# A hybrid decoder layer: where the first FFN weights and the last norms stand among the out-projection's products, and which engine takes the samples' small FFN steps

## The chip, the cores and the metric

The kernel runs on one core of one Trainium2 chip. The metric is device time in microseconds (us) of one execution. A core has five engines that each work through their own queue in order: TensorE (PE, matrix products, with PEld for its weight loads), VectorE (DVE), ScalarE (ACT), GpSimd (POOL) and SyncE (SP, which here issues nearly all DMAs).

## What is computed

One layer of a decoder for 2048 prompt tokens and for 32 sample tokens (8 sequences of 4), model width 1024. Four mixers share one input projection; their normed outputs are concatenated, and the rest of the layer is what this change touches:

```python
x = x + jnp.concatenate([ya, yb, yc, yd], axis=-1) @ P['w_out'][l]
hn = rmsnorm(x, P['norm_ffn_g'][l])
x = x + jnp.square(jax.nn.relu(hn @ P['w_up'][l])) @ P['w_down'][l]
...
y_prompt = rmsnorm(h, norm_final_g)
```

All is float32 in and out. The kernel makes each fp32 operand into a high and a low fp16 part and does three fp16 products for one fp32 product.

## The kernel before

**Planner.** The program is written against a framework that plans the order of the instructions on each engine when the kernel is built: an instruction written earlier has priority over one written later, and the planner, with its own estimates of durations, lets each engine take the ready instruction of the highest priority. On the chip that order is fixed, so an engine stands still when the instruction at its head isn't ready. Tiles of one tag share a number of buffers (`bufs`); a tile's first writer waits until the last user of the buffer's previous tile is done.

**Out-projection** (`outproj`, from L1864). Prompt tokens are worked on in units of 256 (a pair of 128-token tiles), two units to a block; blocks 0 and 1 go first and are put aside in DRAM, then blocks 2 and 3 (`BLOCKS[0]`) follow. `load` (L1883) fetches a unit's `cat` (tag `cat`, 2 buffers) and its residual `x2`. `product(cat, x2, t, m)` (L1892) makes 512 of the 1024 output columns of one token tile: 48 products of 256 columns into one PSUM tile `px` (2 buffers), then two adds on DVE (L1898). `m = 0` uses the weight tiles `W[0]`, `W[1]`, `m = 2` uses `W[2]`, `W[3]`; these four tiles fill the four buffers of tag `w`, in which the FFN's `wd` and `wdT` tiles must later find a place. For block 3 all four `m = 0` products stand ahead of all four `m = 2` products, and after them both units' `norm_pair`.

**Norm** (`norm_pair`, L1939). For each token tile: sum of squares on ACT (L1950), reciprocal root on POOL (L150, L151), scaling on DVE (L1953, `xn`), eight transposes on PE (L144), copies from PSUM on ACT (L1958) into `xt`. `combine` (L1960) makes the operand forms of a Strassen-like product of 2x2 blocks: four subtractions into `tt` (L1964 to L1967; for block 3 L1965 is on POOL), then high parts on ACT (L1971) and low parts on DVE (L1972) into `hn`. For block 3 `xt` and `tt` are tiles of tag `cat`, so they take the two buffers that the units' `cat` leave; the FFN's `fr` (L2076) has the same tag and comes after them.

**FFN weights.** `ffn_wu(s, c)` (L2008) loads 256 columns of `w_up` into a staging tile `ws` (2 buffers, shared with the norms of block 2), and for `s = 0` finds a power-of-two scale: squares on ACT (L183), a product with ones on PE (`pd<-w_ss,ones`), one POOL step (L188) and small DVE steps (L187, L155, L191, L192). Then it makes high parts on ACT (L176) and low parts on DVE (L177), with four POOL steps on `ws` between (L2027 to L2030). `ffn_wd(s, c)` (L2036) does the same for 256 rows of `w_down` (POOL steps L2053 to L2056, tiles `wd` and `wdT`).

**FFN** (`ffn`, L2061). Pass `s = 0` works on blocks 2 and 3 and the samples, pass `s = 1` on blocks 0 and 1. In a pass, 16 chunks `c` of 256 hidden columns, each for both blocks: 64 steps in all. `up` makes seven products of 12 matrix instructions each, evacuated by ACT (L2089, L2107) and DVE (L2092) into `fr`, then relu and square on ACT (L2111, L2112), and the forms `ht` of the second Strassen-like product (POOL L2129 to L2131, L2137, L2139, L2140; ACT and DVE). `down` makes 14 groups of three 512-column products and adds them into the residual on DVE (L2182), scaled by `f`. A step's `up` is written ahead of the previous step's `down`. The samples ride along with block 2 (272 instead of 256 columns); for them `hs` holds high and low parts of the squared values: four ACT steps (L2119) and four DVE steps (L2120) per chunk, read by 32 small products (`pd<-hs,wd`) that DVE adds to `accs` (L2157). `f` is made once per chunk and pass from the scales by three DVE steps on one column (L2220 to L2222).

**Order around the change.** `ffn_wu(0, 0)` is written ahead of block 2's norms. `ffn_wd(0, 0)` is the first thing in `ffn`, after both norms of block 3. `ffn_wu(0, 1)` comes in the main loop at `n = 0`, after `up` of the first two steps.

Of the kernel before, what the change touches and what calls it, by code (L numbers as in the profile page):

```python
# [10 lines left out]
F16 = mybir.dt.float16  # L11
BF = mybir.dt.bfloat16
I32 = mybir.dt.int32
AF = mybir.ActivationFunctionType
OP = mybir.AluOpType
# [8 lines left out]
NS = 32  # L24
# [3 lines left out]
BLOCKS = [(2, 3), (0, 1)]  # L28
# [75 lines left out]
class K:  # L104
# [1763 lines left out]
    def outproj(self, ctx, mix):  # L1868

        nc, A = self.nc, self.A  # L1870
        W = self.Wo
        self.fp = ctx.enter_context(self.pool("ffn", 1))
        self.hnp = ctx.enter_context(self.pool("hn0", 1))
        gb, self.ish, g8 = self.gain_row(self.hnp, A["norm_ffn_g"], "ffn", True)

        self.xp = {BLOCKS[0][0]: ctx.enter_context(self.pool("x2a", 1))}
        rot = mix.enter_context(self.pool("rot", 2, "right"))

        self.xD = {b: [self.dr.tile([128, 2 * D], F32, name=f"x2D{b}{i}") for i in range(2)] for b in BLOCKS[1]}
        self.hD = {b: [self.dr.tile([128, 7 * 4 * 2 * 128], F16, name=f"hnD{b}{i}") for i in range(2)] for b in BLOCKS[1]}  # L1880

        def load(u, b, i):

            cat = self.hnp.tile([128, 8, 2, 256], F16, name="cat", tag="cat", bufs=2)
            for g in range(4):
                nc.sync.dma_start(cat[:, 2 * g:2 * g + 2], self.catD[g][u // 2][:, :, :, u % 2 * 256:u % 2 * 256 + 256])
            x2 = self.xp[b].tile([128, 2, D], F32, name="x2", tag=f"x2{b}{i}")
            nc.sync.dma_start(x2, A["x_prompt"][0, u * 256:(u + 1) * 256, :].rearrange("(i p) d -> p i d", p=128))
            return cat, x2

        def product(cat, x2, i, m):

            p = self.ps("mm", [128, 512])
            for mm in range(2):
                self.proj_tok(p[:, mm * 256:(mm + 1) * 256], cat[:, :, :, i * 128:i * 128 + 128], W[m + mm][0], 0, 256)
            for mm in range(2):
                o = x2[:, i, (m + mm) * 256:(m + mm + 1) * 256]
                nc.vector.scalar_tensor_tensor(o, p[:, mm * 256:(mm + 1) * 256], W[m + mm][1], o, op0=OP.mult, op1=OP.add)  # L1898

        for b in BLOCKS[1]:  # L1900
            for i in range(2):
                cat, x2 = load(2 * b + i, BLOCKS[0][0], i)
                for t in range(2):
                    for m in (0, 2):
                        product(cat, x2, t, m)
                hn = rot.tile([128, 7, 4, 2, 128], F16, name="hnr")
                self.norm_pair(x2, gb, hn)
                nc.sync.dma_start(self.xD[b][i], x2.rearrange("p t d -> p (t d)"))
                nc.sync.dma_start(self.hD[b][i], hn.rearrange("p o k a n -> p (o k a n)"))
        first = [load(2 * BLOCKS[0][0] + i, BLOCKS[0][0], i) for i in range(2)]  # L1910
        for i, t, m in ((i, t, m) for i in range(2) for t in range(2) for m in (0, 2)):
            product(*first[i], t, m)
        mix.close()
        self.xp[BLOCKS[0][1]] = ctx.enter_context(self.pool("x2b", 1, "right"))
        self.hp = ctx.enter_context(self.pool("hn", 1))
        self.bank["t"] = "b"
        self.wup = ctx.enter_context(self.pool("wu", 2, "right"))
        self.wts = {}
        self.accs = self.hp.tile([128, 8, NS], F32, name="accs")
        self.wsc = self.hp.tile([128, 2, 4096 // FC, 2], F32, name="wsc")  # L1920
        self.x2, self.hn = {}, {}
        for b in BLOCKS[0]:
            n = 128 + (NS // 4 if b == BLOCKS[0][0] else 0)
            hn = self.hp.tile([128, 2, 7, 4, 2, n], F16, name=f"hn{b}", tag=f"hn{b}")
            prs = first
            if b != BLOCKS[0][0]:
                prs = [load(2 * b + i, b, i) for i in range(2)]

                for i, t, m in ((i, t, m) for m in (0, 2) for i in range(2) for t in range(2)):
                    product(*prs[i], t, m)  # L1930
            if b == BLOCKS[0][0]:
                self.ffn_wu(0, 0)
            for i in range(2):
                self.norm_pair(prs[i][1], gb, hn[:, i, :, :, :, 0:128], b == BLOCKS[0][1])
            if b == BLOCKS[0][0]:
                self.out_sample(hn, g8)
            self.x2[b] = [x2 for _, x2 in prs]
            self.hn[b] = hn

# [121 lines left out]
    def ffn(self):  # L2061
        nc, A, O = self.nc, self.A, self.O
        RS = float(0.7 * 2.0 ** -20)
# [1 line left out]
        nc.sync.dma_start(gf, dram(A["norm_final_g"], 0, [[0, 128], [1, D]]))  # L2065
        accs = self.accs
        NC_ = 4096 // FC
        self.ffn_wd(0, 0)

        def up(s, c, b):  # L2070

# [2 lines left out]
            n = X.shape[5]  # L2074
            N = 2 * n
            r2 = self.hnp.tile([128, 7, N], F32, name="fr", tag="cat", bufs=2)  # L2076
            C, S = r2[:, 0:4], r2[:, 4:7]
            p, q, r = self.ps("s", [128, 512]), self.ps("mm", [128, 512]), self.ps("mm", [128, 512])
# [29 lines left out]
            for i in range(4):  # L2108
                x = C[:, i, :]
# [2 lines left out]
                nc.scalar.activation(x, x, AF.Square)  # L2112
            hs = None
            if n > 128:
                hs = self.hp.tile([128, 2, 2, 2, 2, 8], F16, name="hs", bufs=2)
                for m in range(2):
                    for t in range(2):
                        x = C[:, ((0, 2), (3, 1))[m][t], :].rearrange("p (i n) -> p i n", i=2)[:, :, 128:]
                        nc.scalar.activation(hs[:, m, 0, t], x, AF.Copy)  # L2119
                        nc.vector.tensor_sub(hs[:, m, 1, t], x, hs[:, m, 0, t])  # L2120


            ht = self.fp.tile([128, 7, 2, N], F16, name="ht", tag="xn", bufs=2)
# [20 lines left out]
        def down(s, c, b, ht, f):  # L2144
            ht, hs = ht
            n = ht.shape[3] // 2
            wd = self.wts[s, c][2]
            if hs is not None:
                p = self.ps("o", [128, 8, 2, NS])
                for m in range(8):  # L2150
                    for k in range(2):

                        x, o = hs[:, k].rearrange("p a t i n -> p (a t i n)"), p[:, m].rearrange("p a n -> p (a n)")
                        self.mm(o, wd[:, k, 0, m * 128:(m + 1) * 128], x, start=m + k == 0, stop=False)
                        self.mm(o[:, 0:NS], wd[:, k, 1, m * 128:(m + 1) * 128], x[:, 0:NS], start=False, stop=k == 1)
                for a in range(2):
                    nc.vector.scalar_tensor_tensor(accs, p[:, :, a, :], f, accs, op0=OP.mult, op1=OP.add)  # L2157
                if c == NC_ - 1:
                    self.ffn_sample_out(gf)
            for i in range(2):  # L2160
                if (s, c) in PLAIN:
                    down_plain(wd, self.x2[b][i], ht[:, :, :, i * n:i * n + 128], f)
                else:
                    down_pair(wd, self.wts[s, c][3], self.x2[b][i], ht[:, :, :, i * n:i * n + 128], f)
                if c == NC_ - 1:
                    for t in range(2):
                        tok = (4 * b + 2 * i + t) * 128
                        self.final(self.x2[b][i][:, t, :], 128, gf, O["y_prompt"][0, tok:tok + 128, :],
                                   (b, i) != (BLOCKS[1][1], 1))
# [42 lines left out]
        steps = [(s, c, b) for s in range(2) for c in range(NC_) for b in BLOCKS[s]]  # L2212
        first = BLOCKS[0][0]
        ht, f = up(*steps[0]), None
        for n, (s, c, b) in enumerate(steps):
            if b == BLOCKS[s][0]:

                _, iu, _, _, idn = self.wts[s, c]
                f = self.col("ff", bufs=4)
                nc.vector.tensor_scalar(f, iu, self.ish, 1.0 / RS, op0=OP.mult, op1=OP.mult)  # L2220
                nc.vector.tensor_mul(f, f, f)
                nc.vector.tensor_mul(f, f, idn)  # L2222
            nx = up(*steps[n + 1]) if n + 1 < len(steps) else None
            if (s, c) != (1, NC_ - 1):
                (self.ffn_wu if b == BLOCKS[s][0] else self.ffn_wd)(s + (c + 1) // NC_, (c + 1) % NC_)
            down(s, c, b, ht, f)
            if s == 0 and c == NC_ - 1:
                self.ffn_load(b, BLOCKS[1][BLOCKS[0].index(b)])
            ht = nx
# [66 lines left out]
```

## Time and profile before

| | |
|---|---|
| time, median of 3 runs | 2596.7 us (2593.09 to 2603.4) |
| the profiled execution | 2600.62 us |
| its span, first to last instruction | 2598.8 us |
| mean granted TensorE clock over the span | 0.974 of full speed |
| out-projection ends, FFN begins | about 1293 us |
| pass 0 of the FFN ends | about 1957 us |

A view by windows gives the busy time of each engine in a stretch, with its instruction count in brackets, then the granted TensorE clock (PEclk, 1.00 is full speed), the share of time that the DMA engines were busy and what they moved. Timeline rows give start, duration, engine, line, operation, output and inputs, count, and in square brackets how long the engine had been idle just before and what released it. Rows by line give busy time and mean nanoseconds, then the idle time of the engine just before such instructions and what ended it.

### The profile page before, as it was taken

To read this page: it belongs to the slowest core of one execution; us is meant where nothing else is said; L and a number is where in the kernel's file an instruction comes from. 1 tells how busy PE (TensorE), PEld (TensorE's weight loads), DVE (VectorE), ACT (ScalarE), POOL (GpSimd) and SP (SyncE) were. 2 spreads that over 40 slices of the span, in tenths; PEclk is the share of its full clock that TensorE was granted. 3 is DMA by queue.
4 is the path that set the end of the run, shared out by engine and by line. 5 is a ranking of instruction groups with operands and counts; after the bars stand their busy time and mean duration, and the time that the engine had idled before them with its cause. 6 is when DMAs were issued, how large, how long until landed. Compare 5 with 4: busy or idle time off the path is not lost.

```text
span 2598.8 us, 51309 instructions
## 1 busy us (share of the span) xinstructions
PE 2433.9 (94%) x20492; PEld 1660.2 (64%) x20492; DVE 2007.0 (77%) x3742; ACT 1312.5 (51%) x2449; POOL 1214.8 (47%) x1265
## 2 busy tenths in 40 slices
PE   6989999999999899999979999999998999999997
PEld 5875554454467677689856666666665666666664
DVE  5666667875566777654689998898997898999996
ACT  6544333033346677562455565556556554555554
POOL 3503122223214566540255555556556665666652
PEclk9989999999999998999989999999999999999999
DMA  6333416879722433355111111121136211121101
GB/s 190 96 73 94 89 40 199 301 256 336 254 87 75 132 104 97 99 175 212 52 41 50 60 55 50 49 66 33 55 126 216 77 59 50 56 66 49 66 33 65
DMA packets 209464, 278.31 MB, mean 107 GB/s; under 512 B 42852, under 2 KB 177121, under 8 KB 198952
## 3 DMA queue, kind: packets, MB, share of 16 engines
q1 hardware_dynamic: 199848, 207.40, 25.7%
q0 software_dynamic: 9376, 67.64, 7.2%
q8 instruction: 160, 2.62, 0.4%
q14 instruction: 80, 0.66, 0.1%
HBM read 217.85 MB, written 54.29 MB: 105 GB/s over the span
## 4 chain that ended last, share of the span: by engine, by line
PE 53%; DVE 17%; POOL 13%; ACT 6%; issue 5%; DMA 5%; SPq 1%; POOLq 0%; DVEq 0%; ACTq 0%
PE pb L140 26%; PE px L140 24%; DVE x L2182 4%; DVE wu L177 2%; PE pd L140 2%; DVE wd L177 1%; PE pb L144 1%; POOL ht L2137 1%; DMA ws<-in_w_up_dram 1%; POOL ws L2030 1%; POOL ws L2028 1%; POOL ht L2139 1%; POOL ws L2029 1%; DVE wdT L177 1%; ACT wdT L176 1%
## 5 line engine op out<-in xcount | busy, mean ns | idle before, releaser
L140 PEld LDWEIGHTS <-wu 128*128 128x128 f16 x5376 | 529.7, 99 | 225.9 <-issue 40.9
L2182 DVE SCALAR_TENSOR_TENSOR x<-pb,ff,x 128x512 f32<-128x512 f32 x840 | 591.3, 740 | 27.0 <-PE pb L140 23.0
L140 PE MATMUL px<-hn,wu 128*128 128x256 f16 (+1 forms) x3072 | 427.2, 276 | 16.6 <-DVE hn L1972 7.6
L140 PEld LDWEIGHTS <-ht 128*128 128x128 f16 x2712 | 264.1, 98 | 231.5 <-issue 25.0
L140 PE MATMUL pb<-wdT,ht 128*128 128x512 f16 x1440 | 379.6, 381 | 16.0 <-DVE x L2182 9.1
L140 PE MATMUL px<-xT,w 128*128 128x512 f16 (+1 forms) x1968 | 368.0, 338 | 1.5 <-ACT da L722 1.2
L140 PE MATMUL pb<-wd,ht 128*128 128x512 f16 x1272 | 336.0, 381 | 6.5 <-DVE x L2182 4.9
L140 PE MATMUL pb<-hn,wu 128*128 128x256 f16 (+1 forms) x2304 | 303.3, 277 | 16.7 <-DVE x L2182 8.4
L140 PEld LDWEIGHTS <-w 128*128 128x128 f16 x2160 | 167.4, 99 | 184.8 <-issue 25.1
L900 POOL TENSOR_TENSOR pl<-P,ph 128x512 f16<-128x512 f32 (+3 forms) x160 | 166.4, 1049 | 159.6 <-ACT ph L897 65.7
L176 ACT ACTIVATE wu<-ws,wsc 128x1024 f16<-128x1024 f32 (+1 forms) x128 | 129.4, 1036 | 128.7 <-POOL ws L2030 76.6
L177 DVE SCALAR_TENSOR_TENSOR wu<-ws,wsc,wu 128x1024 f16<-128x1024 f32 (+1 forms) x128 | 169.9, 1341 | 17.5 <-ACT wu L176 17.3
L140 PE MATMUL px<-w,cat 128*128 128x256 f16 x1536 | 180.2, 274 | 3.3 <-DMA cat<-cat 3.3
L140 PE MATMUL px<-w,xT 128*128 128x128 f16 (+1 forms) x2400 | 155.2, 223 | 15.5 <-DVE xT L402 8.0
L140 PEld LDWEIGHTS <-cat 128*128 128x128 f16 x1536 | 149.6, 98 | 25.7 <-DMA cat<-cat 3.4
L140 PEld LDWEIGHTS <-xT 128*128 128x128 f16 (+1 forms) x2672 | 151.3, 100 | 21.9 <-DVE xT L402 11.3
L893 ACT ACTIVATE P<-pb,nck,cc 128x512 f32<-128x512 f32 (+3 forms) x160 | 112.2, 710 | 76.0 <-PE pb L140 73.4
L2134 ACT ACTIVATE ht<-fr 128x1024 f16<-128x1024 f32 (+1 forms) x60 | 64.2, 1070 | 160.3 <-POOL fr L2140 160.2
L2137 POOL TENSOR_TENSOR ht<-fr,ht 128x512 f16<-128x512 f32 (+1 forms) x60 | 83.2, 1386 | 113.7 <-ACT ht L2136 112.4
L2053 POOL TENSOR_TENSOR ws<-ws 128x512 f32<-128x512 f32 x30 | 40.5, 1349 | 187.7 <-DVE wd L177 187.7
L862 DVE TENSOR_REDUCE mx<-pb 128x1 f32<-128x512 f32 (+3 forms) x160 | 94.9, 607 | 41.5 <-PE pb L140 40.2
L2111 ACT ACTIVATE fr<-fr 128x256 f32<-128x256 f32 (+1 forms) x192 | 77.0, 414 | 93.4 <-DVE fr L2092 92.5
(713 smaller groups left out, 4650.1 us busy)
## 6 DMA issues: line engine op xcount, KB each, us to landing
ws<-in_w_up_dram SPq DMA_DIRECT2D x32, 1024.0 KB
ws<-in_w_down_dram SPq DMA_DIRECT2D x32, 1024.0 KB
ws<-in_w_in_dram SPq DMA_DIRECT2D x22, 512.0 KB
x<-in_x_prompt_dram SPq DMA_DIRECT2D x16, 512.0 KB
cat<-cat SPq DMA_DIRECT2D x32, 256.0 KB
x<-in_x_prompt_dram SPq DMA_DIRECT2D x8, 1024.0 KB
out_y_prompt_dram<-x SPq DMA_DIRECT2D x32, 256.0 KB
hnD<-hnr SPq DMA_DIRECT2D x4, 1792.0 KB
```

The lines of the kernel that those rows point to most:

```text
L140: self.nc.tensor.matmul(out, lhsT, rhs, start=start, stop=stop, skip_group_check=True)
L144: self.nc.tensor.transpose(out, in_, self.ident[:n, :n])
L176: self.nc.scalar.activation(hi, x, AF.Copy, scale=sc)
L177: self.nc.vector.scalar_tensor_tensor(lo, x, sc, hi, op0=OP.mult, op1=OP.subtract)
L862: nc.vector.tensor_reduce(mx[:, ii, jb:jb + 1], s[:, :n], axis=AX.X, op=OP.max)
L893: nc.scalar.activation(P[:, :n], s[:, :n], AF.Exp, bias=nck[:, j, h, kt:kt + 1], scale=cc[:, h // 2:h // 2 + 1])
L900: (nc.gpsimd if 1 else nc.vector).tensor_sub(pl[:, :n], P[:, :n], ph[:, :n])
L2053: nc.gpsimd.tensor_sub(B11, B12, B11)
L2111: nc.scalar.activation(x, x, AF.Relu)
L2134: nc.scalar.activation(ht[:, o:o + m, 0, :], x, AF.Copy)
L2137: nc.gpsimd.tensor_sub(ht[:, 0:2, 1, :], C[:, 0:2, :], ht[:, 0:2, 0, :])
L2182: nc.vector.scalar_tensor_tensor(o, p, f, o, op0=OP.mult, op1=OP.add)
```

## The change

Four things. In `outproj`, block 3's steps are written in another order: four `m = 0` products, `ffn_wd(0, 0)`, the first unit's two `m = 2` products, its norm, `ffn_wu(0, 1)`, the second unit's two `m = 2` products, its norm. Accordingly `ffn_wd(0, 0)` leaves `ffn`, and the main loop no longer makes `ffn_wu(0, 1)` at `n = 0`. In `up`, the samples' high and low parts are made for two of the four blocks at a time, so two ACT steps and two low-part steps per chunk in place of four and four; the low-part steps go from DVE to POOL, and the order of the dimensions in `hs` is changed to suit, with `down`'s small products reading the same columns. The three steps for `f` go from DVE to POOL.

```diff
@@ outproj
             prs = first
-            if b != BLOCKS[0][0]:
-                prs = [load(2 * b + i, b, i) for i in range(2)]
-
-                for i, t, m in ((i, t, m) for m in (0, 2) for i in range(2) for t in range(2)):
-                    product(*prs[i], t, m)
             if b == BLOCKS[0][0]:
                 self.ffn_wu(0, 0)
-            for i in range(2):
-                self.norm_pair(prs[i][1], gb, hn[:, i, :, :, :, 0:128], b == BLOCKS[0][1])
-            if b == BLOCKS[0][0]:
+                for i in range(2):
+                    self.norm_pair(prs[i][1], gb, hn[:, i, :, :, :, 0:128])
                 self.out_sample(hn, g8)
+            else:
+                prs = [load(2 * b + i, b, i) for i in range(2)]
+                for i, t in ((i, t) for i in range(2) for t in range(2)):
+                    product(*prs[i], t, 0)
+                self.ffn_wd(0, 0)
+                for i in range(2):
+                    for t in range(2):
+                        product(*prs[i], t, 2)
+                    self.norm_pair(prs[i][1], gb, hn[:, i, :, :, :, 0:128], True)
+                    if i == 0:
+                        self.ffn_wu(0, 1)
@@ ffn
-        self.ffn_wd(0, 0)
@@ up
-                hs = self.hp.tile([128, 2, 2, 2, 2, 8], F16, name="hs", bufs=2)
-                for m in range(2):
-                    for t in range(2):
-                        x = C[:, ((0, 2), (3, 1))[m][t], :].rearrange("p (i n) -> p i n", i=2)[:, :, 128:]
-                        nc.scalar.activation(hs[:, m, 0, t], x, AF.Copy)
-                        nc.vector.tensor_sub(hs[:, m, 1, t], x, hs[:, m, 0, t])
+                hs = self.hp.tile([128, 2, 4, 2, 8], F16, name="hs", bufs=2)
+                for q in range(2):
+                    x = C[:, 2 * q:2 * q + 2, :].rearrange("p o (i n) -> p o i n", i=2)[:, :, :, 128:]
+                    d = [hs[:, a, q:4 - q:3 - 2 * q] for a in range(2)]
+                    nc.scalar.activation(d[0], x, AF.Copy)
+                    nc.gpsimd.tensor_sub(d[1], x, d[0])
@@ main loop
-                nc.vector.tensor_scalar(f, iu, self.ish, 1.0 / RS, op0=OP.mult, op1=OP.mult)
-                nc.vector.tensor_mul(f, f, f)
-                nc.vector.tensor_mul(f, f, idn)
+                nc.gpsimd.tensor_scalar(f, iu, self.ish, 1.0 / RS, op0=OP.mult, op1=OP.mult)
+                nc.gpsimd.tensor_mul(f, f, f)
+                nc.gpsimd.tensor_mul(f, f, idn)
             nx = up(*steps[n + 1]) if n + 1 < len(steps) else None
-            if (s, c) != (1, NC_ - 1):
+            if (s, c) != (1, NC_ - 1) and n > 0:
```

## Rows read from the trace of the kernel before

**Rows 1.** The page's part 1: busy time, share of the span and instructions by engine.

```profile
PE 2433.9 (94%) x20492; PEld 1660.2 (64%) x20492; DVE 2007.0 (77%) x3742; ACT 1312.5 (51%) x2449; POOL 1214.8 (47%) x1265
```

**Rows 2.** Windows: turn to the FFN, most of pass 0, most of pass 1.

```profile
1293.00:1375.00 82.00, 59.38 (x435) 43.21 (x434) 67.00 (x85) 50.09 (x85) 49.42 (x40) 0.88 0.12 39
1375.00:1957.00 582.00, 554.86 (x4125) 371.12 (x4125) 528.83 (x847) 337.88 (x598) 328.00 (x306) 0.99 0.19 61
2050.00:2560.00 510.00, 504.45 (x3451) 338.32 (x3450) 466.54 (x617) 253.77 (x469) 304.87 (x261) 0.99 0.16 52
```

**Rows 3.** Windows: last out-projection products, and the two stretches after them.

```profile
1278.00:1293.00 15.00, 15.00 (x140) 13.47 (x138) 4.91 (x8) 6.08 (x8) 1.46 (x4) 1.00 0.24 71
1293.00:1300.00 7.00, 4.48 (x40) 3.96 (x38) 4.79 (x11) 6.53 (x10) 3.69 (x5) 1.00 0.02 4
1300.00:1328.40 28.40, 12.10 (x61) 8.70 (x62) 27.93 (x22) 14.59 (x17) 19.72 (x12) 0.64 0.06 25
```

**Rows 4.** Timeline, 1278 to 1295 us: `wd`'s squares, a scaled token tile, then PE.

```profile
1278.35 1.91 ACT L183 ACTIVATE wd<-ws 128x2048 f16<-128x2048 f32 x1 [2.71 <-DMA ws<-in_w_down_dram]
...
1287.01 1.28 DVE L1953 SCALAR_TENSOR_TENSOR xn<-x,n_rstd,gb 128x1024 f32<-128x1024 f32 x1 [2.61 <-POOL n_rstd L151]
...
1292.83 1.91 PE L144 MATMUL pb<-cst,xn 128*128 128x128 f32 x16
...
1294.58 0.28 PE L140 MATMUL pd<-w_ss,ones 128*128 128x1 f32 x2
```

**Rows 5.** Timeline, 1317 to 1329 us: PE's longest waits and the first evacuations into `fr`.

```profile
1317.85 2.29 PE L140 MATMUL px<-hn,wu 128*128 128x256 f16 x10 [7.55 <-DVE hn L1972]
...
1324.73 0.38 ACT L2089 ACTIVATE fr<-px 128x272 f32<-128x272 f32 x1
...
1324.87 3.14 PE L140 MATMUL pb<-hn,wu 128*128 128x256 f16 x14 [4.74 <-ACT hn L1971]
```

**Rows 6.** By line, 1375 to 1957 us, PE: what it waited for before products.

```profile
L140 PE MATMUL pb<-wdT,ht 128*128 128x512 f16 x684 | 180.1, 380 | 8.6 <-DVE x L2182 8.4
L140 PE MATMUL pb<-hn,wu 128*128 128x256 f16 (+1 forms) x1044 | 140.4, 279 | 10.4 <-DVE x L2182 7.4 <-ACT fr L2089 2.9
L140 PE MATMUL pb<-wd,ht 128*128 128x512 f16 x519 | 138.0, 379 | 5.2 <-DVE x L2182 4.9
```

**Rows 7.** By line, whole span: low parts of weights on DVE.

```profile
L177 DVE SCALAR_TENSOR_TENSOR wu<-ws,wsc,wu 128x1024 f16<-128x1024 f32 (+1 forms) x128 | 169.9, 1341 | 17.5 <-ACT wu L176 17.3
...
L177 DVE SCALAR_TENSOR_TENSOR wdT<-ws,wsc,wdT 128x2048 f16<-128x2048 f32 x30 | 74.1, 2471 | 10.5 <-ACT wdT L176 10.5
```

**Rows 8.** By line, whole span: DVE steps that the change moves.

```profile
L2120 DVE TENSOR_TENSOR hs<-fr,hs 128x16 f16<-128x16 f32 x64 | 33.6, 531 | 11.8 <-ACT hs L2119 11.8
...
L2221 DVE TENSOR_TENSOR ff<-ff 128x1 f32<-128x1 f32 x32 | 15.6, 490 | 0.2
...
L2222 DVE TENSOR_TENSOR ff<-ff,wsc 128x1 f32<-128x1 f32 x32 | 13.2, 412 | 0.3
```

**Rows 9.** By line, whole span: one of the POOL steps on staged weights.

```profile
L2030 POOL TENSOR_TENSOR ws<-ws 128x512 f32<-128x512 f32 x32 | 58.1, 1816 | 1.7
```

**Rows 10.** Timeline of PE in an earlier block: a norm's transposes among products.

```profile
1202.63 0.60 PE L144 MATMUL pd<-cst,xn 128*128 128x128 f32 x4
```

**Rows 11.** By tile (`ff`, `hs`): nanoseconds min/median/max, first and last start.

```profile
L2220 DVE TENSOR_SCALAR ff<-wsc,inv_ffn x32: 195/202/215, 1242.1 to 2456.7; 128x1 f32<-128x1 f32 x32
...
L2120 DVE TENSOR_TENSOR hs<-fr,hs x64: 157/513/1267, 1331.3 to 1946.6; 128x16 f16<-128x16 f32 x64
```

**Rows 12.** Small two-input POOL steps: by tile (min/median/max), and by line and shape.

```profile
L2261 POOL TENSOR_TENSOR fi_rs<-fi_ssq x17: 183/193/2241, 1977.0 to 2591.5; 128x1 f32<-128x1 f32 x16, 32x1 f32<-32x1 f32 x1
...
L1231 POOL TENSOR_TENSOR qCe<-qeA,xbcS 128x64 f32<-128x64 f32 x2 | 0.6, 320 | 0.0
```

**Rows 13.** Timeline, 1377 us: last low part of a chunk's `hs`, then its product.

```profile
1377.20 0.16 DVE L2120 TENSOR_TENSOR hs<-fr,hs 128x16 f16<-128x16 f32 x1
...
1377.97 0.75 PE L140 MATMUL pd<-hs,wd 128*128 128x64 f16 x22
```

More of the change, by code (lines that the diff above doesn't have):

```diff
@@ L2151, in down @@
                     for k in range(2):
-                        x, o = hs[:, k].rearrange("p a t i n -> p (a t i n)"), p[:, m].rearrange("p a n -> p (a n)")
+                        x, o = hs[:, :, 2 * k:2 * k + 2].rearrange("p a t i n -> p a (t i n)"), p[:, m]
                         self.mm(o, wd[:, k, 0, m * 128:(m + 1) * 128], x, start=m + k == 0, stop=False)
-                        self.mm(o[:, 0:NS], wd[:, k, 1, m * 128:(m + 1) * 128], x[:, 0:NS], start=False, stop=k == 1)
+                        self.mm(o[:, 0], wd[:, k, 1, m * 128:(m + 1) * 128], x[:, 0], start=False, stop=k == 1)
                 for a in range(2):
```

## The prediction

> **What bounds the kernel now.** First, part 1 of the page: TensorE is busy for 94% of the span and no other compute engine for more than 77% [rows 1], so time is to be gained only where PE stands still or runs at the low clock. The windows say where that is [rows 2]. In the turn from out-projection to FFN, 1293 to 1375 us, PE is busy for 59.4 of 82 us: 22.6 us idle, at a mean granted clock of 0.88. In pass 0 of the FFN it is idle for 582 - 554.9 = 27.1 us, in pass 1 for 510 - 504.5 = 5.5 us. The change touches just these three stretches.
>
> The turn, read closer: while the last products run, 1278 to 1293, PE is full, but DVE works for 4.9 us of 15, ACT for 6.1 and POOL for 1.5 [rows 3]. Right after it is the other way round: from 1300 to 1328.4 DVE is busy for 27.9 of 28.4 us and PE for 12.1, at a mean granted clock of 0.64, a mixture of its two levels (1.2 and 2.4 GHz) after PE had begun to wait. The timeline shows why so little was done ahead. The squares of `wd` were finished at 1280.3 and the second scaled token tile of the first unit at 1288.3, but the transposes and the product with ones that go on from them stand on PE at 1292.8 and 1294.6, behind all products [rows 4]. After that PE waits 7.55 us for low parts of `hn` and 4.74 us for high parts, and the first evacuation into `fr` is at 1324.73 [rows 5], since `fr` takes a buffer that `xt` has to leave.
>
> In pass 0 three rows hold 24.2 us of PE's idle time, and 8.4 + 7.4 + 4.9 = 20.7 us of it ended with the residual adds of L2182 on DVE, which free PSUM [rows 6].
>
> **The change part by part.**
>
> *Order of block 3.* No instruction is removed; some 20 us of DVE, ACT and POOL work gets a higher priority than the last products, or than half of them. Of DVE's work after 1293 four things can be done before: the split of `wd` (2.5 us by the 2471 ns of a step of that size), the low parts of the first unit from `xt` and the first splits of `wu` (0, 1) (two steps each of 1.34 us or less), and the split of `wdT` when its POOL steps are through [rows 7]. That is 6 to 9 us, and DVE has 15 - 4.9 = 10 us free there [rows 3]. `tt` can't come forward: its buffer is the second unit's `cat`, in use until the last product. The 28.4 us in which DVE is full shrink by these 6 to 9. Two more things come off. The steps for `f`, on one column, average 490 and 412 ns [rows 8]; a few of them fall into this stretch, and they leave DVE: 2 us. And DVE steps are stretched where POOL steps run beside them; with half of POOL's eight steps on `ws` (1.8 us each, after the mean of L2030 [rows 9]) done before 1293, fewer are: I estimate 3 to 6 us. Sum 11 to 17 us. The most that the turn can give is PE's idle time from 1293 to 1328.4, (7 - 4.5) + (28.4 - 12.1) = 18.8 us [rows 3], and a little of the low clock: 20 us. It can't all go, since the second unit's last tile still has its add, squares, root, scaling, transposes, copies and subtractions after the last product. I take 15 us; bounds 5 and 20.
>
> What it costs: PE does the first unit's transposes (1.9 us) and two products with ones (0.3 us each) [rows 4] among the products instead of behind them, the same work. That such steps don't make PE wait shows in blocks 0 and 1, where four transposes take 0.60 us among products that go on at once [rows 10]. The adds L1898 may come up to one split (2.5 us) late behind the new DVE work; 140 matrix instructions fill 15 us [rows 3], so a product of 48 lasts 5.1 us and there are two PSUM buffers: covered; without that cover it would cost 2 us for each of four products. On SP the loads of `ws` keep their order: they wait for staging buffers that block 2's norm holds, and that of `w_down` had landed by 1278.35 [rows 4], so no DMA passes another that matters; those of chunk 1 follow earlier. On POOL both weights' eight steps move ahead of the second unit's reciprocal roots, which lie on the chain just named: up to 4 x 1.8 = 7 us late (rival 2).
>
> *Small steps to POOL.* DVE loses 64 steps on `hs` (33.6 us) and 96 on `f` (15.6 + 13.2 us [rows 8], and 32 x 0.202 = 6.5 us [rows 11]), 68.9 us in all. All of `hs` and half of `f` lie in pass 0, 51 us, so that DVE's 528.8 of 582 us there [rows 2] become about 480, from 91% to 82%. ACT's copies for `hs` halve as well. POOL gets 32 steps of 128x32 and 96 of 128x1, which the trace doesn't show as such: the nearest are 193 ns for 128x1 with two inputs, 320 ns for 128x64, and 2241 ns for one that was held up [rows 12]. I take 0.25 to 0.6 us each, near the first two since the shapes are theirs; that is 32 to 77 us on an engine that is busy for 328 of 582 and 305 of 510 us [rows 2]; it has room.
>
> What that gives PE: at the most the 20.7 us that ended with DVE. But DVE is idle for 9% in pass 1 as well (466.5 of 510), and PE is idle there for 1% only, so it is bursts and not the mean load that stop PE; a DVE relieved by a tenth shortens a part of the bursts. I take half, 10 us; bounds 0 and 21, and below nothing for new waits on POOL (rival 3). In pass 1 `f` alone moves; of 5.5 us idle I take 1, bounds -2 and 4. The wait for `f` itself costs nothing while it is made a whole step ahead of the first add that reads it; behind it on DVE stand the residual adds, and if it were late they would be too.
>
> A rule speaks against this part. The Trainium skill (GPSIMD Engine Reference, 4.1 Engine selection) wants elementwise steps of two inputs on VectorE, as GpSimd takes about twice as long. Set against the trace: alone a DVE step on `hs` takes 157 ns, but its median is 513 and its longest 1267 [rows 11], so what DVE gives up is three times its own work. By the rule's factor the moved steps would cost POOL an estimated 0.3 us each, 40 us in all, which leaves the sum as it is. A second rule of the Trainium skill (SBUF — State Buffer, Who interferes with whom) says that a VectorE step with two SBUF inputs and a GpSimd step that reads SBUF exclude each other for the whole of an instruction. The 157 to 1267 ns agree with it; by that rule the wait may move to POOL along with the step, which is rival 3.
>
> *Sum.* 15 + 10 + 1 = 26 us. The profiled execution took 2600.6 us (1.8 more than its span), so it would become 2574.6; the median of the runs, 2596.7, is 3.9 us lower, which gives 2570.7, rounded 2571.
>
> **The rivals.**
>
> 1. *The loop gains nothing.* PE's waits in pass 0 are bursts from the weight splits of L177, which stay. For it: pass 1 shows the same DVE load without the waits [rows 2]. Against it: 20.7 us of PE's waits end with DVE [rows 6], and a tenth of its work goes. Then 15 us remain: 2582.
>
> 2. *POOL's queue or the planner eats the turn.* POOL's eight steps stand ahead of the second unit's roots, or PE's order leaves the transposes late as before. For it: POOL is busy for 19.7 us in the 28.4 in which PE waits [rows 3]. Against it: the program now writes the first unit's norm and `wd` ahead of products, and in earlier blocks such steps do stand among products [rows 10]. Then the turn gives 15 - 7 or less, say 4, and with 6 from the loop the time is 2596.7 - 10 = 2587.
>
> 3. *POOL gates the samples' products; slower than before.* PE takes the products on `hs` 0.6 us after DVE's last low part [rows 13], so there is little slack in PE's order. On POOL the low parts may stand behind steps on `ws` of 1.8 us each [rows 9], which wait in turn for DVE's splits of up to 2.5 us [rows 7]. If they come late by one and a half such steps, 2.7 us, in each of 16 chunks, PE loses 43 us, less the 15 of the turn: 2625. It decides from a lateness of (15 + 13) / 16 = 1.75 us a chunk. Against it: the planner knows POOL's order too and places the products accordingly; the lateness would have to be what its estimates miss.
>
> 4. *Both gains near their ends*, 20 + 20 + 2: 2555.
>
> **How the numbers follow.** A measurement of this kernel can tell about 0.5%, 13 us, from no change: faster is below 2583.7, slower above 2609.7. Forecast (2571, its own range 2556 to 2584) 0.55; rival 1 (2582) 0.17; rival 2 (2587) 0.10; rival 3 (2625) 0.10; rival 4 (2555) 0.08. Faster: nearly all of the first, half of rival 1, all of rival 4, 0.70; same: the rest of these and rival 2, 0.20; slower: 0.10. The range of 8 in 10 goes from 2552, just below the best case, to 2597, which takes in the eaten turn and leaves out the slow case.
>
> **What would show it.** Right: among the products before 1293 stand transposes and the products with ones of `wd` and `wu` (0, 1); the first evacuation into `fr` comes near 1310; PE's idle time from 1293 to 1375 falls from 22.6 to about 9 us; DVE's busy time falls by some 65 us over the span, and PE's idle time in pass 0 from 27 to about 17 us. Wrong: PE waits in the midst of the last products for a scale or a root; POOL's steps on `ws` stand ahead of the second unit's roots; PE waits for POOL before `pd<-hs,wd`; or DVE's load falls and PE's waits in pass 0 don't.

## The result, and the profile after

The changed kernel takes 2639.95 us (median; 2632.39 to 2644.52) against 2598.11 for the kernel before on the same chip: 1.0153 times as long, 95% interval 1.0125 to 1.0181. It is slower, by 1.5%; the forecast was 2571, with a range of 2552 to 2597.

Lines of the changed kernel lie 6 or 7 higher in the out-projection and the FFN (L2140 is now L2147). Part 1 of its page, answering [rows 1]:

```profile
PE 2436.2 (93%) x20492; PEld 1661.2 (63%) x20492; DVE 1967.4 (75%) x3582; ACT 1308.6 (50%) x2417; POOL 1280.4 (49%) x1393
```

Windows of the kernel after, the stretches of [rows 2]:

```profile
1293.00:1375.00 82.00, 64.03 (x477) 45.96 (x478) 62.96 (x76) 44.72 (x76) 45.03 (x42) 0.88 0.18 58
1375.00:1957.00 582.00, 556.15 (x4099) 370.54 (x4097) 499.83 (x739) 332.25 (x566) 364.05 (x382) 0.99 0.19 64
2050.00:2560.00 510.00, 472.19 (x3175) 314.47 (x3174) 430.43 (x544) 241.42 (x443) 316.36 (x282) 0.98 0.15 51
```

VectorE did lose work, 39.6 us of it (some 65 were forecast), and GpSimd took 65.6 more. But in pass 1, where almost nothing was changed, TensorE's idle time went from 5.5 to 37.8 of 510 us.

Windows of fixed times mix two things, since the code ahead of the change, the same in both, took 1231.1 us in one profiled run and 1239.6 in the other. So the stages are measured from marks of their own. The first mark is the weight load of the first weight scale's product with ones (`pd<-w_ss,ones`) in the out-projection; from it the times to the first evacuation into `fr` and to the first product on `hs` are counted. Pass 0 is taken from the first to the last product on `hs`. Pass 1 is taken from the first to the last residual add of the plain chunks (the last chunk of each pass, made without the Strassen-like forms). For the kernel after:

```profile
L140 PE MATMUL pd<-hs,wd x512: 177/184/193, 1334.5 to 1946.8; 128*128 128x64 f16 x86, 128*128 128x32 f16 x85
L2216 DVE SCALAR_TENSOR_TENSOR x<-pb,ff,x x32: 730/743/751, 1949.6 to 2621.6; 128x512 f32<-128x512 f32 x32
```

The marks of all kernels, in us; the last column is counted in the planned order of instructions: in how many of pass 1's 30 half chunks (one block's `up`) a weight step on `ws` stands on GpSimd between the last sum of `fr` (L2140, after L2147) and the sum before it; steps of `f` can stand there too.

| kernel | to the first mark | to first `fr` | to first `hs` | pass 0 | pass 1 | weight step ahead of the sum |
|---|---|---|---|---|---|---|
| before | 1239.6 | 85.1 | 102.6 | 613.5 | 631.3 | 0 |
| after | 1231.1 | 85.4 | 103.4 | 612.3 | 672.0 | 11 |
| e1_f_pool | 1241.8 | 83.3 | 102.6 | 618.3 | 660.6 | 7 |
| e2_f_back | 1234.6 | 85.0 | 102.2 | 608.8 | 672.5 | 13 |
| e3_hs_only | 1248.0 | 85.1 | 104.2 | 606.7 | 673.9 | 13 |
| e4_order_only | 1240.3 | 85.0 | 102.2 | 610.9 | 632.1 | 0 |
| e9_before_edge | 1236.9 | 85.1 | 102.8 | 613.7 | 642.4 | 0 |
| e5_hs_edge | 1232.2 | 85.1 | 104.0 | 607.0 | 643.9 | 0 |
| e6_after_edge | 1233.0 | 85.6 | 102.8 | 612.0 | 655.6 | 0 |
| e7_order_hs_edge | 1232.2 | 84.9 | 102.2 | 609.0 | 643.7 | 0 |
| e10_before_early | 1245.2 | 85.1 | 102.7 | 613.3 | 653.5 | 9 |
| e11_before_lock | 1233.9 | 85.1 | 102.7 | 613.6 | 624.9 | 0 |
| e13_order_hs_lock | 1230.9 | 85.0 | 102.3 | 609.1 | 637.9 | 0 |
| e14_after_lock | 1239.9 | 85.5 | 102.7 | 612.2 | 651.0 | 0 |
| e16_turn_only | 1231.5 | 79.8 | 99.0 | 612.0 | 622.4 | 0 |
| e18_turn_hs_lock | 1237.9 | 79.7 | 101.9 | 608.8 | 635.0 | 0 |
| e17_after_sum_dve | 1232.2 | 85.5 | 102.7 | 611.4 | 665.5 | (sum on DVE) |

So the turn lost 0.8 us, pass 0 gained 1.2, and pass 1 lost 40.7, nearly all of the 41.8 between the medians.

Each row is one profiled execution. Three pairs of kernels have the same order of instructions in pass 1 (`e2_f_back` and `e3_hs_only`, `e5_hs_edge` and `e7_order_hs_edge`, `e13_order_hs_lock` and `e18_turn_hs_lock`); their pass 1 differs by 1.4, 0.2 and 2.9 us, so a difference of up to 3 us there shows nothing.

Where it went in pass 1: what PE waited for from 2050 to 2560 (total, times, longest), after:

```profile
PE px L140 <- ACT fr L2095: 24.9, 6, 4.6
PE pb L140 <- ACT fr L2095: 8.0, 5, 3.2
PE pb L140 <- DVE x L2189: 4.4, 11, 1.0
```

In the kernel before these were 3.4, 0.4 and 1.0. One such wait, in the timeline of GpSimd, ScalarE and TensorE after:

```profile
2317.11 2.24 POOL L2063 TENSOR_TENSOR ws<-ws 128x512 f32<-128x512 f32 x1
2319.31 0.64 POOL L2228 TENSOR_TENSOR ff<-ff 128x1 f32<-128x1 f32 x1
2320.03 0.19 POOL L2229 TENSOR_TENSOR ff<-ff,wsc 128x1 f32<-128x1 f32 x1
2320.17 0.73 POOL L2136 TENSOR_TENSOR fr<-fr 128x256 f32<-128x256 f32 x1
2320.86 0.73 POOL L2138 TENSOR_TENSOR fr<-fr 128x256 f32<-128x256 f32 x1
2321.54 2.76 POOL L2146 TENSOR_TENSOR ht<-fr,ht 128x256 f16<-128x256 f32 x1
2324.26 0.72 POOL L2137 TENSOR_TENSOR fr<-fr 128x256 f32<-128x256 f32 x1
2324.95 1.26 POOL L2034 TENSOR_TENSOR ws<-ws 128x512 f32<-128x512 f32 x1
2326.17 0.73 POOL L2147 TENSOR_TENSOR fr<-fr 128x256 f32<-128x256 f32 x1
...
2326.93 1.06 ACT L2141 ACTIVATE ht<-fr 128x1024 f16<-128x1024 f32 x1 [5.54 <-POOL fr L2147]
2327.89 0.37 ACT L2095 ACTIVATE fr<-px 128x256 f32<-128x256 f32 x1
...
2328.31 2.56 PE L140 MATMUL px<-hn,wu 128*128 128x256 f16 x12 [4.62 <-ACT fr L2095]
```

Read it upwards from PE: it waits for a PSUM buffer that ACT's evacuation frees; the evacuation is queued behind the high parts of `ht`, which have waited 5.54 us for the last sum of `fr`; and on POOL a weight step, L2034, stands ahead of that sum. Its 1.26 us are only a part of the delay: another weight step (L2063, 2.24 us) and two steps of `f` stand ahead of the first sum, and the low part L2146, 2.76 us long here, has come among the sums. In the kernel before the low part takes 0.67 us and is done, the four sums run through, and the weight steps follow:

```profile
2312.68 0.67 POOL L2139 TENSOR_TENSOR ht<-fr,ht 128x256 f16<-128x256 f32 x1
2315.94 0.73 POOL L2129 TENSOR_TENSOR fr<-fr 128x256 f32<-128x256 f32 x1 [2.59 <-ACT fr L2112]
2316.63 0.73 POOL L2131 TENSOR_TENSOR fr<-fr 128x256 f32<-128x256 f32 x1
2317.32 1.80 POOL L2130 TENSOR_TENSOR fr<-fr 128x256 f32<-128x256 f32 x1
2319.20 1.06 POOL L2140 TENSOR_TENSOR fr<-fr 128x256 f32<-128x256 f32 x1
2320.22 1.27 POOL L2027 TENSOR_TENSOR ws<-ws 128x512 f32<-128x512 f32 x1
```

PE's next twelve instructions in the kernel after take 2.56 us, where twelve of the same shape took 1.47 at 2312.91: from 2328.3 to 2330.9 the granted clock was 0.54, near the lower of its two levels. So this wait costs more than its length.

### The profile page after: what moved, and what is told of

It reads as the page before. It is cut to its first block, busy times and chain, and to the rows that moved or that the text cites. A ratio compares the mean times of both kernels' runs of the same rounds, so it can differ in the third digit from the quotient of the medians.

```text
span 2630.6 us, 51236 instructions
## 1 busy us (share of the span) xinstructions
PE 2436.2 (93%) x20492; PEld 1661.2 (63%) x20492; DVE 1967.4 (75%) x3582; ACT 1308.6 (50%) x2417; POOL 1280.4 (49%) x1393
## 4 chain that ended last, share of the span: by engine, by line
PE 46%; POOL 22%; DVE 14%; ACT 8%; DMA 5%; issue 4%; SPq 1%; DVEq 0%; POOLq 0%; ACTq 0%
PE px L140 22%; PE pb L140 21%; DVE x L2189 2%; DVE wu L177 2%; PE pd L140 2%; POOL ws L2061 2%; DVE wd L177 2%; POOL ws L2063 2%; POOL ws L2034 1%; POOL ht L2146 1%; POOL ws L2062 1%; POOL ws L2060 1%; POOL ht L2144 1%; POOL fr L2136 1%; POOL ws L2037 1%
## 5 line engine op out<-in xcount | busy, mean ns | idle before, releaser
L140 PE MATMUL pb<-wd,ht 128*128 128x512 f16 x1272 | 330.7, 379 | 10.1 <-DVE x L2189 8.7
L140 PE MATMUL pb<-hn,wu 128*128 128x256 f16 (+1 forms) x2304 | 308.2, 278 | 21.0 <-ACT fr L2095 13.8
L140 PEld LDWEIGHTS <-xT 128*128 128x128 f16 (+1 forms) x2672 | 150.5, 100 | 22.4 <-DVE xT L402 11.6
L2144 POOL TENSOR_TENSOR ht<-fr,ht 128x512 f16<-128x512 f32 (+1 forms) x60 | 73.2, 1221 | 130.8 <-ACT ht L2143 119.6
L2117 ACT ACTIVATE fr<-fr 128x256 f32<-128x256 f32 (+1 forms) x192 | 76.5, 414 | 101.9 <-DVE fr L2098 100.1
```

Source lines behind the costliest of these rows:

```text
L140: self.nc.tensor.matmul(out, lhsT, rhs, start=start, stop=stop, skip_group_check=True)
L2117: nc.scalar.activation(x, x, AF.Relu)
L2144: nc.gpsimd.tensor_sub(ht[:, 0:2, 1, :], C[:, 0:2, :], ht[:, 0:2, 0, :])
```

## The experiments

Theory A: the steps that were moved to GpSimd hold up its queue in pass 1. Theory B: what they hold matters little; with them the planner writes another order, and in it weight steps come ahead of the last sum. (The planned order of PE, ACT and VectorE changes along with GpSimd's in most of these kernels; the last column of the table follows one feature of it. "Chunk" stands for the half of one in some of the expectations, where they count places in the order.)

**The parts alone.** `e1_f_pool` is the kernel before with the three lines of `f` as in the change; `e2_f_back` the change with them on `nc.vector` again; `e3_hs_only` the kernel before with the edit of `hs`; `e4_order_only` the kernel before with block 3's new order.

> The kernel before with the three steps of the samples' factor f on GpSimd and nothing else changed. The loss of the whole change lay in pass 1 (from the first residual add of that pass to the last 672.0 us, against 631.3 before). Theory A, the three steps themselves (their time and the time they hold GpSimd's turn ahead of the relu sums) cost it: +35 to +41 us, about 2636, and every chunk of pass 1 takes about 41 us instead of 36.7. Theory B, the planner's new order costs it: a weight step of the next chunk stands ahead of the last sum of fr, and ScalarE's next tile and the evacuations behind it wait for that sum. In this kernel's planned order that is so only in the last half of pass 1: the first eight chunks then keep about 36.7 us, the later ones take about 41, in all +15 to +22 us, about 2617.

Measured 2634.92, ratio 1.0128 [1.0101, 1.0155].

> The whole change with the three steps of f back on VectorE. Theory A (f's steps on GpSimd): the loss goes, 2590 to 2600. Theory B (planned order): in pass 1 a weight step stands ahead of the last sum of fr in ten chunks of fifteen here too, though no f step is on GpSimd; it stays 20 to 40 us above the kernel before, 2620 to 2640.

Measured 2634.02, ratio 1.0143 [1.0107, 1.0178].

> The kernel before with only the samples' low halves (hs) moved to GpSimd, two larger steps instead of four. hs exists in pass 0 alone, so in pass 1 no instruction is added or removed; only the planner's order differs there. Theory A: pass 1 as before, 631 us; in all 2585 to 2600, the lower end if VectorE's relief in pass 0 counts as the prediction had it (10 us). Theory B: pass 1 loses 20 to 40 us as in the whole change, 2615 to 2640, by order alone.

Measured 2637.83, ratio 1.0140 [1.0113, 1.0166].

> The kernel before with only the turn reordered: the first weights and the last block's norm between the last out-projection products, hs and f as before. Its planned order in pass 1 is that of the kernel before. Both theories: pass 1 stays 631 us. The trace of the whole change says that the turn gained nothing (a 10.0 us wait for the second unit's xn ate it): 2595 to 2602. If the turn as the prediction had it were right and only the other parts hid it: 2580 to 2590.

Measured 2594.0, ratio 0.9979 [0.9962, 0.9996].

`hs` exists in pass 0 only. Its move took 6.8 us off pass 0, and put 42.6 on pass 1, without one instruction more or less there. That ends theory A for `hs`. Its GpSimd timeline has the same picture as after:

```profile
2297.33 0.72 POOL L2130 TENSOR_TENSOR fr<-fr 128x256 f32<-128x256 f32 x1
2298.01 1.27 POOL L2027 TENSOR_TENSOR ws<-ws 128x512 f32<-128x512 f32 x1
2299.24 2.77 POOL L2140 TENSOR_TENSOR fr<-fr 128x256 f32<-128x256 f32 x1
```

`e2_f_back` says the same of `f`: with it on VectorE the loss stays. In `e4_order_only` pass 1 and the turn are as before, and pass 0 gains 2.6.

In `e1_f_pool` the planned order turns in the middle of pass 1. From the first to the fifteenth last sum, with `f` on POOL and no weight step ahead, 261.4 us pass (2007.5 to 2268.9), and 262.5 in the kernel before; from there to the last sum 302.6, and 272.4. All of the 29.3 us that pass 1 lost lies where weight steps stand ahead. Counted from last sum to last sum, a chunk of the kernel before takes 36.7 us there; here it takes 39.5 to 42.5, and in the kernel after 39.5 and 42.5 in turn. The size was more than expected (36 and not 15 to 22): pass 1 alone lost 29.3, and pass 0 another 4.8.

**The order held.** A constraint makes POOL steps written inside a block stand behind a given POOL instruction, in the order only:

```diff
-            nc.gpsimd.tensor_sub(A12, A12, S[:, 1, :])
+            self.z[s, c, b] = nc.gpsimd.tensor_sub(A12, A12, S[:, 1, :]).ins
...
+                with self.tc.issue_after(self.z[s, c, b]) if s == 1 and (s, c, b) in self.z else ExitStack():
                     (self.ffn_wu if b == BLOCKS[s][0] else self.ffn_wd)(s + (c + 1) // NC_, (c + 1) % NC_)
```

> The kernel before, with one constraint on the planner in pass 1: the four weight steps that are written at a step of the loop may not stand ahead of that step's last sum of fr on GpSimd. Nothing else changes. It is the control of the three runs beside it: in the kernel before, no weight step of pass 1 stands between a step's sums, so both theories expect pass 1 to stay near 631 us and the time near 2599. The weights come later by up to one step (18 us) than in the kernel before; if a step's products then wait for them, it is slower, and the three others are to be read against this one.

Measured 2611.17, ratio 1.0044 [1.0027, 1.0060].

> The low halves hs on GpSimd (which alone measured 2637.8 us, with 673.9 in pass 1 and 606.7 in pass 0), with the same constraint in pass 1. Theory B (planned order): the loss of pass 1 goes, 631 to 640 us there, and about 2592 to 2600 in all, since pass 0 keeps its gain of 6.8. Rival: what is lost in pass 1 comes from something else that the hs edit brings (a later state of the buffers at the end of pass 0, a lower clock): it stays at 2630 to 2640.

Measured 2603.97, ratio 1.0019 [1.0001, 1.0038].

> The whole change with the same constraint in pass 1. Its three f steps per chunk still stand between a step's sums on GpSimd, in about half of the steps. Theory B with weight steps alone as the cause: pass 1 near 635 us, in all 2590 to 2600. If the f steps matter too (three at up to 2.3 us of a 40 us chunk): pass 1 near 650, in all about 2615.

Measured 2620.63, ratio 1.0080 [1.0053, 1.0108].

> The whole change with f on VectorE and the same constraint in pass 1: the turn's order, hs on GpSimd. By the parts: the turn alone measured 2594.0 (0.998 of before), pass 0 gained 4.7 with hs and the turn; with pass 1 at 631 to 635 that gives 2587 to 2595, below the kernel before. Rival as for the run with hs alone: 2630.

Measured 2606.0, ratio 1.0035 [1.0015, 1.0055].

The control, in which the weights come up to one step later, lost 11.1 us in pass 1; all four took longer than expected. From 2050 to 2560 us PE waits there for residual adds (13.8 us) and for ACT's evacuations (10.0), never for a weight, so how the later weights cost that time isn't shown. Beside the control `hs` on GpSimd costs pass 1 only 1.5 us (643.9 against 642.4) in place of 42.6, no more than two traces of one order differ by. The constraint acts in pass 1 alone, so the loss wasn't a state left over from pass 0. With `f` on GpSimd 12 more are lost (655.6 against 643.7). PE's waits for residual adds are 23.8 us there, against 11.6 in `e7_order_hs_edge`; whether the steps of `f` cost this, as in theory A, or the plan that comes with them isn't separated.

**The order of before, made and broken.** In `e10_before_early` pass 1's weights are written one step earlier, which gives them priority, and a step's POOL work stands behind its own weights. The "lock" kernels have both too, and the weights stand behind the previous step's last sum as well; this one constraint is all that `e11_before_lock` has beyond `e10_before_early`:

```diff
+            if n + 1 < len(steps) and steps[n + 1][0] == 1:
+                if s == 0:
+                    weights(s, c, b)
+                if steps[n + 1][1] < NC_ - 1:
+                    with self.tc.issue_after(self.z[s, c, b]) if (s, c, b) in self.z else ExitStack():
+                        weights(*steps[n + 1])
+                    last = self.wlast
+            with self.tc.issue_after(last) if last else ExitStack():
+                nx = up(*steps[n + 1]) if n + 1 < len(steps) else None
```

> The kernel before, instruction for instruction, but in pass 1 each step's weights are written one step earlier, ahead of that step's products, so that they have priority over them. In the planned order this puts one to three weight steps ahead of the last sum of fr in ten chunks of pass 1, with hs and f on VectorE as before. The test of theory B from the other side: if a weight step ahead of that sum costs a chunk about 4 to 5 us, pass 1 takes 660 to 680 us and the time is 2630 to 2650. If the loss in the whole change needs GpSimd's added work (theory A), it stays within 5 us of the kernel before.

Measured 2627.62, ratio 1.0099 [1.0070, 1.0129].

> As the run beside it, with two constraints on the planner in pass 1: a step's four weight steps stand behind the previous step's last sum of fr, and a step's own sums behind its weight steps. That is the order which the planner found by itself for the kernel before, now fixed. Control for the two runs that follow: both theories 2595 to 2602, pass 1 near 631 us and 36.7 us a chunk. The earlier constraint alone, which let the weights come a step later, cost 11 us.

Measured 2593.3, ratio 0.9978 [0.9960, 0.9995].

> The turn's order and hs on GpSimd, f on VectorE, with the order of pass 1 fixed as in the control. Theory B: pass 1 at 631 to 635 us, pass 0 at 607 to 609 against 613.5, turn as before: 2588 to 2596, below the kernel before by 0.1 to 0.4%. If a part of pass 1's loss stays without a weight step ahead of the sum, it is 2600 or more.

Measured 2603.49, ratio 1.0010 [0.9994, 1.0026].

> The whole change with the order of pass 1 fixed as in the control; f's three steps stay on GpSimd among a step's sums. Theory B: the order gives back 25 to 40 of the 41 us. The run with f alone kept 36.6 us a chunk while f's steps stood among the sums and no weight step did, so pass 1 should be 631 to 640 and the time 2595 to 2605. If f's steps cost what the looser constraint left (pass 1 at 655.6 against 643.9 without them), it stays at 2610 or more.

Measured 2621.75, ratio 1.0087 [1.0058, 1.0116].

`e10_before_early` has nothing of the change in it, and pass 1 loses 22.2 us, with weight steps ahead of the sum in nine half chunks: less than expected, but such an order costs time without the change. `e11_before_lock`, with the one constraint more, has none and takes 28.6 us less. It is also 6.4 below the kernel before in pass 1, so its order isn't quite the one that the planner had found there. Held, pass 1 gets back 34.6 of 41 us without `f` (672.5 to 637.9) and 21.0 with it. It isn't all: over the control `e13_order_hs_lock` still loses 13.0, nearly all before 2350, where PE waits for ACT's evacuations (8.4 us in four waits for `px` from 2050 on); no weight step stands among the sums there either, so the rest of the plan has a share too. With `f` on GpSimd (`e14_after_lock`) 13.1 more are lost, and its time is far above the 2595 to 2605 of theory B.

**The turn, and the way into PE.** `e16_turn_only` has the lock and, of the turn's edit, the interleaving alone:

```diff
                 for i, t in ((i, t) for i in range(2) for t in range(2)):
                     product(*prs[i], t, 0)
-                self.ffn_wd(0, 0)
                 for i in range(2):
                     for t in range(2):
                         product(*prs[i], t, 2)
                     self.norm_pair(prs[i][1], gb, hn[:, i, :, :, :, 0:128], True)
-                    if i == 0:
-                        self.ffn_wu(0, 1)
```

`e18_turn_hs_lock` adds `hs` on GpSimd; `e17_after_sum_dve` is the change with the last sum of pass 1 on `nc.vector`.

> The kernel before with the fixed order of pass 1 (its control measured 2593.3 us), and of the turn's edit only the interleaving: each unit's last products are followed by its norm, while the first w_down and the second w_up weights stay written where the kernel before has them, behind the norms. In the whole change the turn took 85.4 us from the first scale product to the first evacuation of the FFN (85.1 before), with a wait of 10.0 us on the second unit's xn, in front of which GpSimd's and VectorE's weight steps stood. If those weight steps ate the gain, the turn is now shorter by 4 to 10 us (75 to 81), and the time is 2584 to 2590, as far as the first products of hs, which need the later weights, don't take it back. If the turn is bound by the second unit's own norm chain and not by the queues, it stays at 85 and the time at 2593.

Measured 2584.37, ratio 0.9948 [0.9928, 0.9967]: faster than both kernels, and the best of all. Over its control it gains 3.7 us up to the first `hs` and 1.6 in pass 0; the 2.5 in pass 1 are within what one order differs by.

> As the run beside it, with hs on GpSimd as well: the version that the runs so far point to. Pass 0 at 607 to 609 us (hs alone gave 606.7 against 613.5), the turn as in the run beside it, pass 1 between the 624.9 of the control and the 637.9 that the turn with hs left under the same constraints. In all 2584 to 2604; below 2593 if pass 1 stays under 632.

Measured 2600.82, ratio 1.0001 [0.9986, 1.0016]: with `hs` on GpSimd pass 0 gains 3.2 us over `e16_turn_only`, pass 1 loses 12.6, and the first `hs` comes 2.9 later.

> The whole change, no constraint on the planner, with one step moved: in pass 1 the last sum of fr, for which ScalarE and the evacuations behind it wait, is on VectorE (30 steps of about 0.4 us). Weight and f steps still stand between the other sums on GpSimd. If the late last sum is what carries GpSimd's queue into TensorE, pass 1 gives back 20 us or more, 630 to 650, and the time is 2598 to 2618. If the loss comes through another way (the low halves of ht on GpSimd, the weights themselves late, VectorE's 12 us more), pass 1 stays above 660 and the time above 2628.

Measured 2636.96, ratio 1.0146 [1.0130, 1.0161].

Up to the first `fr` the turn shortens by 5.3 us once the weight steps stay behind the norms. In the kernel after, the rows of PE, POOL and DVE around the second unit's norm (answering [rows 5]) show why it had not:

```profile
1288.23 1.55 PE L140 MATMUL px<-hn,wu 128*128 128x272 f16 x12
1293.64 1.41 PE L144 MATMUL pb<-cst,xn 128*128 128x128 f32 x8 [3.86 <-DVE xn L1960]
1305.02 1.94 PE L144 MATMUL pb<-cst,xn 128*128 128x128 f32 x8 [9.97 <-DVE xn L1960]
...
1298.67 1.59 POOL L2036 TENSOR_TENSOR ws<-ws 128x512 f32<-128x512 f32 x1
1300.23 0.99 POOL L151 TENSOR_TENSOR n_rstd<-n_rstd,mhalf 128x1 f32<-128x1 f32 x1
...
1300.74 1.27 DVE L177 SCALAR_TENSOR_TENSOR wu<-ws,wsc,wu 128x1024 f16<-128x1024 f32 x1
1301.93 1.74 DVE L1974 TENSOR_TENSOR tt<-xt,tt 128x512 f32<-128x512 f32 x1
1303.60 1.27 DVE L1960 SCALAR_TENSOR_TENSOR xn<-x,n_rstd,gb 128x1024 f32<-128x1024 f32 x1
```

PE has finished the products 57.3 us after its first mark (53.4 before, with fewer other steps among them), and then waits 9.97 us for the last `xn`: the root L151 is behind a weight step on POOL, and `xn` behind a split and a subtraction on DVE. With the weights behind the norms (`e16_turn_only`) the wait ahead of the last transposes is 3.13, where the kernel before had 4.25 (its row first):

```profile
1303.90 1.97 PE L144 MATMUL pb<-cst,xn 128*128 128x128 f32 x8 [4.25 <-DVE wsc L191]
...
1287.05 1.04 PE L144 MATMUL pb<-cst,xn 128*128 128x128 f32 x8
...
1292.38 1.09 PE L144 MATMUL pb<-cst,xn 128*128 128x128 f32 x8 [3.13 <-DVE w_m L155]
...
1304.37 2.29 PE L140 MATMUL px<-hn,wu 128*128 128x256 f16 x10 [5.18 <-DVE hn L1976]
1311.39 3.14 PE L140 MATMUL pb<-hn,wu 128*128 128x256 f16 x14 [4.72 <-ACT hn L1975]
```

`e17_after_sum_dve` missed: pass 1 takes 665.5 us, 6.5 less than after. PE's waits for ACT's evacuations in that stretch fall from 32.9 to 16.3 us, but those for residual adds rise from 4.4 to 15.8:

```profile
PE pb L140 <- DVE x L2189: 15.8, 13, 2.4
PE px L140 <- ACT fr L2095: 8.7, 6, 1.5
PE pb L140 <- ACT fr L2095: 7.6, 3, 3.6
```

The sum before it (L2137) can still wait behind a weight step on POOL (one of 3.31 us at 2244.23 in this kernel), and VectorE has the added step. So the last sum is at most one way in, not the only one; how the loss divides among the ways stays open.

## Why the prediction was wrong

**Turn, 15 us: nothing.** The observation held: transposes and products with ones stood among the products, from 1271.8 on. The step that failed is the last clause of its cost, the POOL steps "up to 4 x 1.8 = 7 us late" put aside as rival 2, and DVE's splits ahead of the second unit's `xn`, counted as work that only gets out of the way. That rival was the right one for this stage. The size was off too: without the weights in the way the interleaving alone gives 5.3 us, and 3.7 up to the first product on `hs`; PE still waits 5.18 and 4.72 us for `hn`, after 7.55 and 4.74 in [rows 5].

**Pass 0, 10 us: 1.2.** Taken alone `hs` gave 6.8 us, two thirds of the estimate, and took 1.6 more up to its first product. The prediction took 51 us off VectorE in this pass; from the first to the last product on `hs` its busy time fell by 27.6 (555.5 to 527.9). In the kernel after, the waits that end with residual adds fell from 20.7 [rows 6] to 10.4, the half that was forecast; those for `fr` on ACT took their place:

```profile
L140 PE MATMUL px<-hn,wu 128*128 128x256 f16 (+1 forms) x1346 | 191.7, 278 | 12.4 <-ACT fr L2095 10.1 <-DVE fr L2098 1.9 <-ACT fr L2113 0.3
L140 PE MATMUL pb<-wdT,ht 128*128 128x512 f16 x672 | 178.1, 383 | 1.2 <-DVE x L2189 1.2
L140 PE MATMUL pb<-wd,ht 128*128 128x512 f16 x551 | 145.3, 379 | 8.5 <-DVE x L2189 8.5
L140 PE MATMUL pb<-hn,wu 128*128 128x272 f16 (+1 forms) x1008 | 137.3, 277 | 3.7 <-ACT fr L2095 3.0 <-DVE x L2189 0.7
```

`f` on GpSimd costs pass 0 3.0 to 4.8 us wherever two kernels differ by it alone (612.3 and 608.8, 612.0 and 609.0, 618.3 and 613.5). So the sum of both comes out near rival 1, in which the loop gains nothing, but in another way: `f` takes back most of what `hs` gives.

**Pass 1, 1 us gained: 40.7 lost.** The step that failed is "it has room": the moved steps were costed by their time on an engine that is busy for 60%, and the rest of that engine's order was taken as given. Their prices were near (`hs` 245 ns and `f` 191 to 268 ns in the median, held up to 2.29 us), and for `hs` they can't be what pass 1 lost, since it has no step there. What the runs showed in its place is the new order of GpSimd's queue: with `hs` moved, pass 1 loses 42.6 us, and 1.5 (against 642.4) or 13.0 (against 624.9) when the weight steps are held behind the sums. For `f`, 12 to 13 us stay in the held orders. Rival 3 said that POOL would gate PE and make it slower, but at `pd<-hs,wd`, where PE waited 0.0 us in the kernel after (7.5 in `e3_hs_only`); that its 2625 lies nearest to the measured time is luck. In the kernel after PE's waits in pass 1 were for ACT's evacuations for the most part (32.9 of 37.8 us idle from 2050 to 2560), in the pass that has no `hs`; by `e17_after_sum_dve` the last sum ahead of them is not the whole reason, and the rest stays open. The bounds of -2 to 4 for pass 1 came from VectorE's load alone; the only row on GpSimd's order in the loop was a duration [rows 9].

```profile
L2127 POOL TENSOR_TENSOR hs<-fr,hs x32: 235/245/2294, 1328.1 to 1937.7; 128x32 f16<-128x32 f32 x32
...
L2229 POOL TENSOR_TENSOR ff<-ff,wsc x32: 181/191/1304, 1276.4 to 2484.1; 128x1 f32<-128x1 f32 x32
```

The second rule cited from the Trainium skill (SBUF — State Buffer, Who interferes with whom: a two-input step on VectorE and one on GpSimd shut each other out) fits the rows above: the sum that takes 2.77 us in `e3_hs_only`, and 0.73 elsewhere, stands beside a split of weights on VectorE:

```profile
2298.73 2.69 DVE L177 SCALAR_TENSOR_TENSOR wdT<-ws,wsc,wdT 128x2048 f16<-128x2048 f32 x1
```

From 1300 us on no sum of `fr` in the kernels before and after and in `e3_hs_only` takes over 0.79 us without such a two-input step beside it, and with one the longest takes 2.87. So the step that stands in front on GpSimd can cost several times its own time.

## What to carry to other kernels

Where a planner writes the order, an edit's price is not the time of its steps: compare the planned order of every engine over the whole loop, also in passes that the edit doesn't touch, before a gain of some microseconds is counted. An engine that is half idle can still be the gate, if another engine's queue stands behind one step of it; look for who waits for its last step. A constraint on the order costs a few lines and is a cheap way to try an edit apart from its plan, but it needs its own control (here 11 us worse in one form and 6 better in pass 1 in another).

## What was not expected of the hardware

The code ahead of the change, the same in all kernels, took from 1230.9 to 1248.0 us in the profiled runs (why is open), while the stretch from the first mark to the first `fr` was 84.9 to 85.6 us in fourteen kernels, with different plans of it. A part of a few microseconds is to be read from marks within one trace, not from the ends of two.
